# A hybrid token mixer on one core: TensorE's order in the recurrent scan phase written out by a merge of two instruction streams

## The chip, the cores and the metric

The kernel runs on one core of a Trainium2 chip. The metric is the device time of one execution in microseconds (us), as the median of several runs. The engines are TensorE (PE, with its weight loads as PEld), VectorE (DVE), ScalarE (ACT), GpSimd (POOL) and SyncE (SP), which issues the DMA transfers. Each engine takes its instructions strictly in the order in which they stand in the program; what a program fixes is that order and the semaphores that an instruction waits for.

## What is computed

Two layers of a diffusion backbone on 256 latent and 256 context tokens of width 1024, in float32. Each layer runs a half-step SwiGLU, three token mixers side by side (grouped attention, a bidirectional RWKV-7 recurrence, a 2-D neighbourhood attention) whose outputs are gated and merged, and another half-step SwiGLU. The change touches the recurrence:

```python
def rwkv_scan(state0, xs, emit):
    def step(state, inp):
        r_t, w_t, k_t, v_t, a_t, b_t = inp
        sa = jnp.einsum('zbhvk,zbhk->zbhv', state, a_t)
        state = state * w_t[..., None, :] + sa[..., :, None] * b_t[..., None, :] + v_t[..., :, None] * k_t[..., None, :]
        out = jnp.einsum('zbhvk,zbhk->zbhv', state, r_t) if emit else None
        return state, out
    return lax.scan(step, state0, xs)
```

z is the direction (forward, backward), h one of 8 heads of size 64. The context is scanned first, and its final state starts the scan of the latent tokens. In the last layer only the latent outputs are needed.

## The kernel before, in words

The large products (feed-forward, input projection, output projection) are "dense": a float32 product is made of three float32r matmuls of 128x128 weights on 512 or 256 columns (`gemm`, L272 to L274; the same in `quantum`, L773 to L775). These three are called a triple below. ACT and DVE split each loaded weight tile into a high and a low part first (L262, L263).

The mixer of a layer has a **scan phase** (`rwkv`) and an attention phase behind it. In the scan phase the 8 heads are taken as 4 columns of two heads (ct = 0 to 3). For each column there are four stages, each of which needs the one before:

- **prep** (`rwkv_prep`, `rwkv_dir`, `gram`): projections of k, v, r for the column (`proj`, tiles `ps_p`), then for each of the two directions a chain over ACT, POOL and DVE from two small products (`ps_w` L949, `ps_a` L953) to the gram products (`ps_g` L1041) and transposes (`ps_kb` L1011 to L1018).
- **inverse** (`inverse`): blocks of 16x16 are inverted on DVE after a transfer to DRAM and back, then five groups of small products for each direction widen that to 64x64 (`ps_x`, `ps_it`, `ps_iw` in `mm` L1127, and `ps_x`, `ps_w` at L1146, L1154).
- **chain** (`chain_steps`): 8 chunk steps, one after the other; in each, PE makes `ps_z` (L1182), ACT copies it, PE makes `ps_u` (L1203), ACT and DVE copy it, PE makes `ps_h` (L1210), DVE adds it into the next state. Products for the outputs (`ps_oo`, L1191 and L1224) stand beside that. Each of these groups is 4 matmuls of 64 columns; a float32 matmul shows as two records in the trace, so a group is x8.
- **out** (`rwkv_out`): normalisation of the column's output over POOL and DVE, and its gate (`ps_gg` L1241).

To fill PE beside this, `spare_quanta` makes a list of 336 **quanta** of the other input projections (tile `ps_gate`); one quantum is one triple, and 8 make a tile. `fill(n)` writes the next n into the program. 64 quanta in layer 0 and 16 in layer 1 (`LEFT`) are kept for the attention phase. The table `FILL` says after which column how many tiles are written. Within layer 0 all dense matmuls of the phase are on 512 columns; in layer 1, 720 of the 960 of `ps_gate` are on 256.

The order on each engine is set by a scheduler that simulates the program and takes, among what is ready in its simulation, what was written first; `prio` moves a block ahead or behind. The chain has `prio(-30)`, and the fill is written last, so it is ready all the time and goes wherever PE would wait, also into the middle of a group of four.

Of the kernel before, what the change touches and what calls it, by code (L numbers as in the profile page):

```python
# [43 lines left out]
FILL = [[5, 7, 3, 4, 24], [8, 5, 4, 4, 24]]  # L44
# [7 lines left out]
    0, 4, 5, 6, 10, 14, 18, 19, 20, 21, 25, 29, 33)  # L52


class Program:
# [261 lines left out]
    def rstd(self, sqs, n, cols, scale, eps, tag="aux"):  # L317
# [5 lines left out]
        for k, sq in enumerate(sqs):  # L323
            for b in range(n):
# [5 lines left out]
                                in1=self.mhalf[:, 0:n * w].rearrange("p (n w) -> p n w", n=n), op=ALU.pow)  # L330
        bc = self.bank(tag, [P, n * P], "ps_bc")
# [193 lines left out]
    def proj(self, tile_i, full):  # L525

        nc = self.nc
        pt = self.bank("mm", [P, NT], "ps_p")
        for h in range(2):
# [273 lines left out]
    def fill(self, n):  # L803

        for _ in range(min(n, len(self.fq))):
            self.fq.pop(0)()


    def shift(self, i, full, pt=None):

        nc, l = self.nc, self.l
        if pt is None:
            pt = self.proj(T_R + i, full)
# [16 lines left out]
    def rwkv(self):  # L830
# [25 lines left out]
        for h in HALVES:  # L856
            for w, pt in zip(ws, pts):
# [5 lines left out]
        self.gdt = self.shift(T_GD - T_R, tok)  # L863
        nc.scalar.activation(out=self.gdt[:, tok], in_=self.gdt[:, tok], func=AF.Tanh, scale=0.5)
        nc.vector.tensor_scalar(out=self.gdt[:, tok], in0=self.gdt[:, tok], scalar1=0.5, scalar2=0.5,
                                op0=ALU.mult, op1=ALU.add)
        self.fq = self.spare_quanta()
        self.fill_to = self.rp, "gm"
        st = {}
# [19 lines left out]
        self.fill(len(self.fq) - 8 * LEFT[l])  # L889
        return y  # L890

    def rwkv_prep(self, ct, st):
# [6 lines left out]
        pk, pv = self.kv0 if ct == 0 else (None, None)  # L899
        k = self.shift(T_RK - T_R + ct, FULL, pk)  # L900
        yield
        v = self.shift(T_RV - T_R + ct, FULL, pv)
        yield
        r = self.shift(ct, tok)
        yield
        sq = self.t()
        nc.scalar.activation(out=sq, in_=k, func=AF.Square, scale=pr[:, 4, ct:ct + 1])
        bc = self.rstd([sq], 4, self.hsel, 1.0, 1e-12)
# [3 lines left out]
        yield  # L912
# [9 lines left out]
        for p in range(2):  # L922
# [3 lines left out]
            nc.vector.tensor_copy(X[o, :, 1, p, :], pv[o, ::-1, :])  # L926
        st["X"] = X
# [6 lines left out]
        st["bonus"] = bonus  # L934
        st["z"] = []
        for z in range(2):
            yield
            st["z"].append((yield from self.rwkv_dir(ct, z, r, k, kk, lora)))

    def rwkv_dir(self, ct, z, r, k, kk, lora):  # L940
# [10 lines left out]
        nc.scalar.activation(out=sw, in_=pw, func=AF.Tanh, scale=0.5, bias=self.wah[:, l, z, ct:ct + 1])  # L951
        pa = self.bank("aux", [P, NT], "ps_a")
# [18 lines left out]
        yield  # L971
# [25 lines left out]
        yield  # L997
        G = self.gram(z, bk, ar)
        yield
# [6 lines left out]
        for p in range(2):  # L1006
# [15 lines left out]
            kb.append(t)  # L1022
        return dict(ar=ar, kb=kb, G=G, pc=pc)

    def gram(self, z, bk, ar):
# [6 lines left out]
        for jh in (1, 0):  # L1032
# [10 lines left out]
            for p in range(2):  # L1043
# [3 lines left out]
                G[p][jh] = g  # L1047
        return G

# [9 lines left out]
    def inverse(self, dirs):  # L1059
# [40 lines left out]
        for i, t in ((0, R), (1, N)):  # L1100
            nc.sync.dma_start(out=dr[i].rearrange("j z (g s) t -> (j z g) (s t)", s=16), in_=t)
        for z in range(2):
# [29 lines left out]
            nc.scalar.activation(out=X, in_=px, func=AF.Copy)  # L1132
            pt = mm("ps_it", W, X)
            nc.vector.tensor_tensor(out=T, in0=T, in1=pt, op=ALU.add)
            pw = mm("ps_iw", X, W)
            nc.vector.tensor_tensor(out=W, in0=W, in1=pw, op=ALU.add)

# [11 lines left out]
            for p, eng in ((0, nc.scalar), (1, nc.vector)):  # L1149
                self.copy(eng, X[rows(p, b)], px[rows(p, b)])  # L1150
            pw = self.bank("ia", [P, NCH, 32], "ps_w2")
# [12 lines left out]

    def rwkv_chain(self, ct, st):
        po = self.bank("po", [P, NCH, C], "ps_oo")
        return po, self.chain_steps(st, po)

    def chain_steps(self, st, po):
# [5 lines left out]
        for s in range(NCH):  # L1175
# [4 lines left out]
            for z, p in units:  # L1180
                rows = halves[1 - p] if first else slice(0, P)
                ins = nc.tensor.matmul(zp[halves[p], z, :], dirs[z]["G"][p][js[z] // 4][rows, js[z] % 4, 0:C],  # L1182
                                       X[rows, s, z, p, :], start=True, stop=True)
            yield ins
# [264 lines left out]
```

## Time and profile before

| | |
|---|---|
| median of 3 runs | 2931.0 us (2927.77 to 2934.51) |
| the profiled execution's own time | 2933.89 us, of which its span is 2932.1 us |
| mean granted TensorE clock | 0.971 |
| PE busy in the span | 2795.4 us (95%) |
| scan phase of layer 0 | about 463 to 995 us of the span |
| scan phase of layer 1 | about 2118 to 2541 us of the span |

The profile is of one execution. Times in its rows are microseconds from the start of the span; a row of the timeline merges equal instructions that follow each other. Matmuls are pipelined and their ends are modelled, so what one costs is read from start to start, not from its duration. "PEclk" is the granted share of TensorE's full clock: 1.0 is 2.4 GHz, 0.5 is 1.2 GHz.

### The profile page before, as it was taken

To read this page: it belongs to the slowest core of one execution; us is meant where nothing else is said; L and a number is where in the kernel's file an instruction comes from. 1 tells how busy PE (TensorE), PEld (TensorE's weight loads), DVE (VectorE), ACT (ScalarE), POOL (GpSimd) and SP (SyncE) were. 2 spreads that over 40 slices of the span, in tenths; PEclk is the share of its full clock that TensorE was granted. 3 is DMA by queue.
4 is the path that set the end of the run, shared out by engine and by line. 5 is a ranking of instruction groups with operands and counts; after the bars stand their busy time and mean duration, and the time that the engine had idled before them with its cause. 6 is when DMAs were issued, how large, how long until landed. Compare 5 with 4: busy or idle time off the path is not lost. (4 is left out here: it accounts for less than half of the span.)

```text
span 2932.1 us, 48565 instructions
## 1 busy us (share of the span) xinstructions
PE 2795.4 (95%) x19654; PEld 2229.4 (76%) x19654; DVE 1766.0 (60%) x3023; ACT 1068.6 (36%) x1928; POOL 277.6 (9%) x274
## 2 busy tenths in 40 slices
PE   7999999999999899999999999999899999898998
PEld 5788887656666666697888888888876678777998
DVE  4667346756674256757673477633578777485654
ACT  3223235323232246433222333222543433374543
POOL 0000011100000111230000110001210110022000
PEclk8999999999999999999999999999999999799998
DMA  7555343221112433336553365433432224344654
GB/s 277 201 187 170 107 134 105 76 69 44 41 58 73 133 108 110 105 119 215 171 181 106 119 201 183 147 102 107 141 114 69 70 60 119 104 130 138 218 177 144
DMA packets 205311, 376.59 MB, mean 128 GB/s; under 512 B 79776, under 2 KB 109088, under 8 KB 205088
## 3 DMA queue, kind: packets, MB, share of 16 engines
q1 hardware_dynamic: 205088, 373.51, 41.1%
q8 instruction: 154, 2.52, 0.4%
q14 instruction: 69, 0.57, 0.1%
HBM read 340.93 MB, written 31.46 MB: 127 GB/s over the span
## 5 line engine op out<-in xcount | busy, mean ns | idle before, releaser
L262 ACT ACTIVATE whi<-raw 128x1024 fp32r<-128x1024 f32 (+1 forms) x399 | 415.1, 1041 | 1102.5 <-PE ps_o L273 297.5
L263 DVE TENSOR_TENSOR wlo<-raw,whi 128x1024 fp32r<-128x1024 f32 (+1 forms) x399 | 500.4, 1255 | 425.1 <-ACT whi L262 415.8
L195 DVE SCALAR_TENSOR_TENSOR acc<-araw,cs,acc 128x1024 f32<-128x1024 f32 x210 | 260.6, 1279 | 14.3 <-DMA araw<-in_w_ada 14.0
L272 PE MATMUL ps_o<-hh,whi 128*128 128x512 f32 (+1 forms) x770 | 268.8, 349 | 0.0
L274 PE MATMUL ps_o<-hh,wlo 128*128 128x512 f32 (+1 forms) x770 | 268.0, 348 | 0.0
L273 PE MATMUL ps_o<-hl,whi 128*128 128x512 f32 (+1 forms) x770 | 266.6, 346 | 0.0
L272 PE MATMUL ps_fg<-uh,whi 128*128 128x512 f32 (+1 forms) x704 | 255.4, 363 | 7.3 <-ACT whi L262 3.7
L773 PE MATMUL ps_gate<-uh,whi 128*128 128x512 f32 (+1 forms) x672 | 255.6, 380 | 3.1 <-ACT whi L262 3.1
L274 PE MATMUL ps_fu<-uh,wlo 128*128 128x512 f32 (+1 forms) x704 | 251.9, 358 | 5.1 <-DVE wlo L263 5.1
L774 PE MATMUL ps_gate<-ul,whi 128*128 128x512 f32 (+1 forms) x672 | 256.0, 381 | 0.0
L274 PE MATMUL ps_fg<-uh,wlo 128*128 128x512 f32 (+1 forms) x704 | 253.4, 360 | 1.7 <-DVE wlo L263 1.7
L775 PE MATMUL ps_gate<-uh,wlo 128*128 128x512 f32 (+1 forms) x672 | 254.4, 379 | 0.7 <-DVE wlo L263 0.6
L273 PE MATMUL ps_fg<-ul,whi 128*128 128x512 f32 (+1 forms) x704 | 252.7, 359 | 0.1
L272 PE MATMUL ps_fu<-uh,whi 128*128 128x512 f32 (+1 forms) x704 | 251.2, 357 | 0.9 <-ACT whi L262 0.9
L273 PE MATMUL ps_fu<-ul,whi 128*128 128x512 f32 (+1 forms) x704 | 250.9, 356 | 0.0
L272 PEld LDWEIGHTS ps_fg<-uh,whi 128*128 128x128 f32 x704 | 134.8, 191 | 38.3 <-ACT whi L262 12.0
L272 PEld LDWEIGHTS ps_o<-hh,whi 128*128 128x128 f32 x770 | 144.7, 188 | 20.4 <-ACT whi L262 1.7
L273 PEld LDWEIGHTS ps_o<-hl,whi 128*128 128x128 f32 x770 | 144.5, 188 | 20.1
L274 PEld LDWEIGHTS ps_o<-hh,wlo 128*128 128x128 f32 x770 | 144.7, 188 | 18.2
L274 PEld LDWEIGHTS ps_fu<-uh,wlo 128*128 128x128 f32 x704 | 133.7, 190 | 26.6 <-DVE wlo L263 8.0
L773 PEld LDWEIGHTS ps_gate<-uh,whi 128*128 128x128 f32 x672 | 130.2, 194 | 28.3 <-issue 5.7
L274 PEld LDWEIGHTS ps_fg<-uh,wlo 128*128 128x128 f32 x704 | 134.7, 191 | 22.2 <-DVE wlo L263 3.0
(298 smaller groups left out, 5270.2 us busy)
## 6 DMA issues: line engine op xcount, KB each, us to landing
raw<-in_ffn_wi SPq DMA_DIRECT2D x176, 512.0 KB, 3.6
araw<-in_w_ada SPq DMA_DIRECT2D x144, 512.0 KB, 3.8
raw<-in_w_in SPq DMA_DIRECT2D x92, 512.0 KB, 3.7
raw<-in_ffn_wo SPq DMA_DIRECT2D x70, 448.0 KB, 3.3
raw<-in_ffn_wo SPq DMA_DIRECT2D x35, 512.0 KB, 3.5
pd<-fg SPq DMA_DIRECT2D x52, 256.0 KB, 2.0
raw<-in_w_branch SPq DMA_DIRECT2D x24, 512.0 KB, 3.8
praw<-in_w_in SPq DMA_DIRECT2D x44, 256.0 KB, 2.8
```

Source lines behind the costliest of these rows:

```text
L195: nc.vector.scalar_tensor_tensor(out=a, in0=raw, scalar=c, in1=a, op0=ALU.mult, op1=ALU.add)
L262: nc.scalar.activation(out=hi[:, :m], in_=r, func=AF.Copy)
L263: self.lo = nc.vector.tensor_tensor(out=lo[:, :m], in0=r, in1=hi[:, :m].bitcast(F32), op=ALU.subtract)
L272: nc.tensor.matmul(pt, wh, xh[k], start=first and k == 0, stop=False)
L273: nc.tensor.matmul(pt, wh, xl[k], start=False, stop=False)
L274: nc.tensor.matmul(pt, wl, xh[k], start=False, stop=last and k == n - 1)
L773: nc.tensor.matmul(pt, wh, xh, start=k == 0, stop=False)
L774: nc.tensor.matmul(pt, wh, xl, start=False, stop=False)
L775: nc.tensor.matmul(pt, wl, xh, start=False, stop=k == KD - 1)
```

## The change

`rwkv` no longer writes prep, chain and fill one after the other for a scheduler to mix. Two generators, `chains` (chain and out of the columns in turn) and `preps` (projections, prep and inverse of the columns in turn), stop (`yield`) after each whole group of matmuls and say two numbers: what the group costs PE, and how long after it the next group can start. `Streams.step` keeps a clock `t` of the program from these numbers. It takes the chain's next group if its time has come, else the preparation's, else one quantum of the fill; only if the fill has run out does it move the clock on. For the PE alone, a `manual_schedule` block makes the order in which the code writes the order on the engine; the other engines are ordered by the scheduler as before. `FILL` is gone; `LEFT` is as it was. A column's prep waits until the chain two columns back is done; the projections of the next column go beside the chain, a triple at a time. In `rwkv_out` the square goes to the buffer `fg` in place of `t`, and the chain's blocks have priority 200.

```diff
+class Streams:
+    NEAR = 0.3
+    def step(self, streams):
+        live = [g for g in streams if self.ready.get(g, 0.0) is not None]
+        if not live:
+            return False
+        g = next((g for g in live if self.ready.get(g, 0.0) <= self.t + self.NEAR), None)
+        if g is None and self.fill(1):
+            self.t += self.cost
+            return True
+        if g is None:
+            g = min(live, key=lambda g: self.ready[g])
+        self.t = max(self.t, self.ready.get(g, 0.0))
+        try:
+            cost, after = next(g)
+        except StopIteration:
+            self.ready[g] = None
+            return True
+        self.t += cost
+        self.ready[g] = self.t + after
+        return True
...
@@ proj
-            w = [[t[:, P * k:P * k + P] for k in range(4)] for t in (wh, wl)]
-            self.gemm(pt[:, full], w, [t[:, full] for t in self.uh[4 * h:4 * h + 4]],
-                      [t[:, full] for t in self.ul[4 * h:4 * h + 4]], h == 0, h == 1)
+            for k in range(4):
+                c, m = slice(P * k, P * k + P), 4 * h + k
+                self.gemm(pt[:, full], [[wh[:, c]], [wl[:, c]]], [self.uh[m][:, full]], [self.ul[m][:, full]],
+                          m == 0, m == KD - 1)
+                yield cost, 0.0
@@ rwkv
-        for _ in self.rwkv_prep(0, st):
-            pass
-        self.inverse(st["z"])
-        self.fill(8 * FILL[l][0])
-        for ct in range(4):
-            nxt = {}
-            po, chain = self.rwkv_chain(ct, st)
-
-            if ct < 3:
-                for _ in self.rwkv_prep(ct + 1, nxt):
-                    pass
-                self.inverse(nxt["z"])
-            with self.prio(-30):
-                for _ in chain:
-                    pass
-            self.rwkv_out(ct, st, po, y)
-            self.fill(min(8 * FILL[l][1 + ct], len(self.fq) - 8 * LEFT[l]))
-            st = nxt
+        left = 8 * LEFT[l]
+        mix = Streams(lambda n: len(self.fq) > left and self.fill(n), 0.69 if need else 0.45)
...
+            for ct in range(4):
+                yield from self.rwkv_proj(ct, sts[ct])
+
+                while done["chain"] < ct - 2:
+                    yield 0.0, 0.5
+                yield from self.rwkv_prep(ct, sts[ct])
+                yield from self.inverse(sts[ct]["z"])
+                done["prep"] = ct
...
+        streams = [chains(), preps()]
+        with self.tc.manual_schedule(engines={mybir.EngineType.PE}):
+            while mix.step(streams):
+                pass
@@ rwkv_dir (ahead of the gram products)
-        yield
-        G = self.gram(z, bk, ar)
-        yield
+        yield 1.1, 14.0
+        G = yield from self.gram(z, bk, ar)
@@ inverse (behind the transfers to DRAM)
+        yield 0.0, 20.0
@@ inverse (behind each of the first three groups; two more have 0.8, 1.0)
+            yield 1.15, 1.0
@@ chain_steps (behind ps_z, ps_u, and ps_h with ps_oo)
+            yield (0.45, 0.8) if first else (0.9, 0.4)
...
+            yield 0.45, 0.9
...
+            yield (0.9, 1.0) if out else (0.45, 1.4)
```

In the order below, a row is an instruction: its line, its tiles and the size of its output, with a count where equal ones follow each other. PE in layer 0, in the chain of the first column, before: a stretch of one chunk step.

```order
L1203 MATMUL ps_u<-zs,W 64x64
L773 MATMUL ps_gate<-uh,whi 128x512
L774 MATMUL ps_gate<-ul,whi 128x512
L1041 MATMUL ps_g_4748<-ar,bk 64x128 x8
L775 MATMUL ps_gate<-uh,wlo 128x512
L1210 MATMUL ps_h<-X,kb 64x64
L773 MATMUL ps_gate<-uh,whi 128x512
L1210 MATMUL ps_h<-X,kb 64x64
L774 MATMUL ps_gate<-ul,whi 128x512
L1210 MATMUL ps_h<-X,kb 64x64
L1041 MATMUL ps_g_4749<-ar,bk 64x128 x8
```

The last `ps_u` of a step, three of its `ps_h`, and gram products of the next column's prep alternate with single dense matmuls. The same column's chain in the changed kernel (its lines are other numbers):

```order
L1261 MATMUL ps_z<-X,G 64x64 x4
L1269 MATMUL ps_oo<-ar,X 64x64 x4
L305 MATMUL ps_p<-uh,phi 128x512
L306 MATMUL ps_p<-ul,phi 128x512
L307 MATMUL ps_p<-uh,plo 128x512
L1282 MATMUL ps_u<-zs,W 64x64 x4
L305 MATMUL ps_p<-uh,phi 128x512
L306 MATMUL ps_p<-ul,phi 128x512
L307 MATMUL ps_p<-uh,plo 128x512
L1289 MATMUL ps_h<-X,kb 64x64 x4
L1302 MATMUL ps_oo<-G,X 64x64 x4
```

Groups are whole, and dense matmuls come by threes. Counted over a scan phase (from its first `ps_first` to its last `ps_gg`), PE leaves the dense matmuls for small ones 305 times before and 114 times now in layer 0, 187 and 110 times in layer 1.

PE at the end of layer 0's scan phase, before: the last steps of the last column's chain.

```order
L1182 MATMUL ps_z<-X,G 64x64 x4
L1191 MATMUL ps_oo<-ar,X 64x64 x3
L773 MATMUL ps_gate<-uh,whi 128x512
L1203 MATMUL ps_u<-zs,W 64x64 x4
L774 MATMUL ps_gate<-ul,whi 128x512
L775 MATMUL ps_gate<-uh,wlo 128x512
L1224 MATMUL ps_oo<-G,X 64x64
L773 MATMUL ps_gate<-uh,whi 128x512
L1210 MATMUL ps_h<-X,kb 64x64 x4
```

Fill stands between all groups there, and 130 dense matmuls stand behind the last `ps_gg`. The same place in the changed kernel, from the inverse of the last column into its chain:

```order
L1205 MATMUL ps_x<-it 64x64 x16
L1205 MATMUL ps_it<-it,W 64x64 x16
L1205 MATMUL ps_iw<-W,it 64x64 x16
L1227 MATMUL ps_x_8188<-it,G 32x32 x16
L1236 MATMUL ps_w_8208<-W,it 32x32 x16
L1261 MATMUL ps_z<-X,G 64x64 x4
L1282 MATMUL ps_u<-zs,W 64x64 x4
L1289 MATMUL ps_h<-X,kb 64x64 x4
L1302 MATMUL ps_oo<-G,X 64x64 x4
L1261 MATMUL ps_z<-X,G 64x64 x4
```

No dense matmul stands in that row. The fill is used up 39 dense matmuls into the inverse of the third column in layer 0, and 27 dense matmuls into the second direction of the third column's prep in layer 1. From there only the projections beside the third column's chain are left: 160 small matmuls in a row ahead of that chain and 497 behind it in layer 0, 209 and 465 in layer 1.

## Rows read from the trace of the kernel before

**Rows 1.** Windows, both scan phases: start:end, us, PE, PEld, DVE, ACT, POOL busy, PEclk, DMA

```profile
463.00:995.00 532.00, 516.06 (x4637) 354.49 (x4635) 317.14 (x703) 171.46 (x332) 43.46 (x30) 0.99 0.23 67
2118.00:2541.00 423.00, 395.70 (x4463) 308.39 (x4462) 306.74 (x697) 168.58 (x338) 39.43 (x30) 0.95 0.30 85
```

**Rows 2.** Timeline, PE, layer 0: start us, us, engine, line, operation; one group broken up

```profile
637.28 0.39 PE L773 MATMUL ps_gate<-uh,whi 128*128 128x512 f32 x1
637.60 0.32 PE L1203 MATMUL ps_u<-zs,W 64*64 64x64 f32 x2
...
640.24 0.39 PE L775 MATMUL ps_gate<-uh,wlo 128*128 128x512 f32 x1
640.47 0.39 PE L773 MATMUL ps_gate<-uh,whi 128*128 128x512 f32 x1
```

**Rows 3.** Timeline, PE, layer 0: a whole group between dense matmuls

```profile
775.21 0.40 PE L274 MATMUL ps_p<-uh,plo 128*128 128x512 f32 x1
775.54 0.45 PE L1203 MATMUL ps_u<-zs,W 64*64 64x64 f32 x8
...
776.25 0.39 PE L774 MATMUL ps_gate<-ul,whi 128*128 128x512 f32 x1
```

**Rows 4.** Timeline, PE, layer 1: dense matmuls on 256 columns

```profile
2500.18 0.28 PE L775 MATMUL ps_gate<-uh,wlo 128*128 128x256 f32 x1
2500.39 0.33 PE L1203 MATMUL ps_u<-zs,W 64*64 64x64 f32 x2
...
2500.87 0.28 PE L774 MATMUL ps_gate<-ul,whi 128*128 128x256 f32 x1
2500.99 0.29 PE L775 MATMUL ps_gate<-uh,wlo 128*128 128x256 f32 x1
```

**Rows 5.** Timeline, PE: first column's prep, layer 0 (three rows) and layer 1

```profile
484.66 1.02 PE L953 MATMUL ps_a<-sh,lora 64*128 64x512 f32 x2
...
496.31 0.89 PE L1041 MATMUL ps_g<-ar,bk 64*64 64x128 f32 x24 [1.33 <-DVE bk L996]
...
527.58 0.22 PE L1018 MATMUL ps_kb<-c_ident,bk 64*64 64x64 f32 x1
...
2131.09 1.02 PE L953 MATMUL ps_a<-sh,lora 64*128 64x512 f32 x2
...
2172.28 0.22 PE L1018 MATMUL ps_kb<-c_ident,bk 64*64 64x64 f32 x1
```

**Rows 6.** Timeline, PE: an inverse's first product (layer 0; layer 1, first and third column)

```profile
555.92 0.32 PE L1127 MATMUL ps_x<-it 64*64 64x64 f32 x2
...
2202.04 0.33 PE L1127 MATMUL ps_x<-it 64*64 64x64 f32 x2
...
2367.45 0.22 PE L1018 MATMUL ps_kb<-c_ident,bk 64*64 64x64 f32 x1
...
2382.42 0.33 PE L1127 MATMUL ps_x<-it 64*64 64x64 f32 x2
```

**Rows 7.** Timeline, PE and DVE: products of the inverse in layer 0

```profile
562.22 1.15 PE L1127 MATMUL ps_iw<-W,it 64*64 64x64 f32 x32
...
563.41 0.69 DVE L1136 TENSOR_TENSOR W<-W,ps_iw 128x512 f32<-128x512 f32 x1 [1.45 <-PE ps_iw L1127]
...
564.35 0.69 PE L1146 MATMUL ps_x<-it,G 32*32 32x32 f32 x32
```

**Rows 8.** Window and timeline, layer 1: the end of the last chain, without fill

```profile
2520.00:2524.00 4.00, 3.64 (x46) 3.03 (x42) 1.87 (x7) 0.55 (x2) 0.00 (x0) 0.50 0.02 8
...
2518.43 0.70 PE L1182 MATMUL ps_z<-X,G 128*64 128x64 f32 x8
2522.44 0.70 PE L1182 MATMUL ps_z<-X,G 128*64 128x64 f32 x8
```

**Rows 9.** Timeline, layer 1: from the chain's end to the attention phase's first product

```profile
2533.71 0.39 ACT L1232 ACTIVATE yf<-ps_oo 128x256 f32<-128x256 f32 x1 [1.11 <-PE ps_oo L1224]
...
2540.66 0.58 PE L272 MATMUL ps_b<-yh,whi 128*128 128x256 f32 x1 [0.52 <-DVE yf L1242]
```

More of the change, by code (lines that the diff above doesn't have):

```diff
@@ L52, with __init__ @@
     0, 4, 5, 6, 10, 14, 18, 19, 20, 21, 25, 29, 33)
+class Streams:
+    NEAR = 0.3
+    def __init__(self, fill, cost):
+        self.t = 0.0
+        self.fill, self.cost = fill, cost
+        self.ready = {}
+    def step(self, streams):
[17 more added lines that the diff above has]
+        return True
 class Program:
@@ L315, in stats_add, with rstd, rstd_steps @@
             nc.gpsimd.tensor_tensor(out=self.zs[:, h], in0=self.zs[:, h], in1=self.z[m][:, h], op=ALU.add)
-    def rstd(self, sqs, n, cols, scale, eps, tag="aux"):
+    def rstd(self, *args, **kw):
+        steps = self.rstd_steps(*args, **kw)
+        while True:
+            try:
+                next(steps)
+            except StopIteration as e:
+                return e.value
+    def rstd_steps(self, sqs, n, cols, scale, eps, tag="aux", after=3.2):
         nc = self.nc
@@ L330, in rstd @@
                                 in1=self.mhalf[:, 0:n * w].rearrange("p (n w) -> p n w", n=n), op=ALU.pow)
+        yield 1.1, after
         bc = self.bank(tag, [P, n * P], "ps_bc")
@@ L528, in proj @@
         pt = self.bank("mm", [P, NT], "ps_p")
+        cost = 0.69 if full is FULL else 0.36
         for h in range(2):
@@ L803, in fill, with shift @@
     def fill(self, n):
-        for _ in range(min(n, len(self.fq))):
+        n = min(n, len(self.fq))
+        for _ in range(n):
             self.fq.pop(0)()
-    def shift(self, i, full, pt=None):
+        return n
+    def shift(self, i, full, pt):
         nc, l = self.nc, self.l
-        if pt is None:
-            pt = self.proj(T_R + i, full)
         ns = (full.stop - full.start) // SEQ
@@ L889, in rwkv, with preps @@
-        self.fill(len(self.fq) - 8 * LEFT[l])
-        return y
+        sts = [{} for _ in range(4)]
+        done = {"prep": -1, "chain": -1}
+        mix = Streams(lambda n: len(self.fq) > left and self.fill(n), 0.69 if need else 0.45)
+        def preps():
+            pg = yield from self.proj(T_GD, tok)
+            self.gdt = self.shift(T_GD - T_R, tok, pg)
+            nc.scalar.activation(out=self.gdt[:, tok], in_=self.gdt[:, tok], func=AF.Tanh, scale=0.5)
+            nc.vector.tensor_scalar(out=self.gdt[:, tok], in0=self.gdt[:, tok], scalar1=0.5, scalar2=0.5,
+                                    op0=ALU.mult, op1=ALU.add)
+            for ct in range(4):
[5 more added lines that the diff above has]
+                done["prep"] = ct
@@ new lines, in chains @@
+        def chains():
+            for ct in range(4):
+                while done["prep"] < ct:
+                    yield 0.0, 0.5
+                with self.prio(200):
+                    po = self.bank("po", [P, NCH, C], "ps_oo")
+                steps = self.chain_steps(sts[ct], po)
+                while True:
+                    with self.prio(200):
+                        try:
+                            said = next(steps)
+                        except StopIteration:
+                            break
+                    yield said
+                yield from self.rwkv_out(ct, sts[ct], po, y)
+                done["chain"] = ct
@@ new lines, in rwkv, with rwkv_proj @@
+        streams = [chains(), preps()]
+        with self.tc.manual_schedule(engines={mybir.EngineType.PE}):
+            while mix.step(streams):
+                pass
+        self.fill(len(self.fq) - left)
+        return y
+    def rwkv_proj(self, ct, st):
+        tok = self.tok
+        pk, pv = self.kv0 if ct == 0 else (None, None)
+        if pk is None:
+            pk = yield from self.proj(T_RK + ct, FULL)
+        st["k"] = self.shift(T_RK - T_R + ct, FULL, pk)
+        if pv is None:
+            yield 0.0, 1.5
+            pv = yield from self.proj(T_RV + ct, FULL)
+        st["v"] = self.shift(T_RV - T_R + ct, FULL, pv)
+        yield 0.0, 1.5
+        pt = yield from self.proj(T_R + ct, tok)
+        st["r"] = self.shift(ct, tok, pt)
+        yield 0.0, 1.5
@@ L970, in rwkv_dir @@
             last = 0
-        yield
         inv = self.t()
@@ L1047, in gram @@
                 G[p][jh] = g
+            yield 1.7, 1.6
         return G
@@ L1243, in rwkv_out @@
         y.append(os_)
+        yield 1.05 if self.need else 0.5, 0.0
     def mixer(self, l, need, nxt_fn, then):
```

49 lines of the change are left out of this document (20 added, 29 removed).

## The prediction, made before the changed kernel ran

> **What bounds the kernel now.** I read the windows of the two scan phases first, since the change orders nothing else. PE is busy for 516.1 of 532 us in layer 0 and 395.7 of 423 in layer 1 [rows 1]: it waits for 15.9 and 27.3 us, and DVE, next, is busy for 317 and 307. So in these phases PE's own instruction stream sets the end, and the time is the price of that stream plus what it waits. The reader is to see two things next. The timeline shows what it costs PE to go from dense matmuls to a small one and back [rows 2 to 4]. And the rows of single stages show how long a column takes from prep to out when PE is not the limit [rows 5 to 9]; before, that hardly matters, since fill stands in every gap, up to the last column's out and behind it in layer 0.
>
> **What the change gives back: crossings.** A broken group: from 637.28 to 640.47, 3.19 us, PE does six dense matmuls and four single `ps_u` (the rows left out alternate in the same way) [rows 2]. Six dense at 0.23 each, the distance of the last two rows, are 1.38, so the four cost 1.81. A whole group: from 775.21 to 776.25, 1.04 us, it does two dense (0.46) and the same four `ps_u`, which so cost 0.58 [rows 3]. Three crossings less are worth 1.23, or 0.41 each. In layer 1, beside 256 columns, two dense at 0.12 and one `ps_u` take 0.69 from 2500.18 to 2500.87, so one single is 0.45, against a quarter of 0.58: 0.31 each [rows 4]. The order has 191 crossings less in layer 0 and 77 less in layer 1: 191 x 0.41 + 77 x 0.31 = 78 + 24 = 102 us. Bounds: 0.31 for all is 83, 0.41 for all 110. PE's waits of 15.9 and 27.3 go into the new sum as well and are taken off here, and some 5 us of layer 1, where the end of the last chain ran at a clock of 0.50 [rows 8] and stays as slow: 48. Together 150 us to gain, if PE never waited.
>
> **What the change takes: cover.** The dense matmuls are as many as before; the clock of the program only deals them out. It deals 60 to 87 of them into each gap that the code says (14 and 20 us), and then has none left: the whole last column and a part of the third run bare. PE waits out there what a column takes, less its own small matmuls, which are paid before as well.
>
> The last column, stage by stage. Prep, from the end of the first `ps_a` to the last `ps_kb`: 485.68 to 527.80, 42.1 us, and 2132.11 to 2172.50, 40.4 [rows 5]. PE did fill beside it, but the chain of ACT, POOL and DVE set these times, so 41. The transfer stage of the inverse, from that `ps_kb` to the first product: 28.1 and 29.5 in the first columns, where projections' splits stood in the same queues, 15.0 at the least (2367.45 + 0.22 to 2382.42), where its masks had run ahead [rows 5, 6]. Bare it has neither; I take 22, the middle. The products: ten groups, three of 1.15 and two of 0.69 for each direction, and after each a copy of 0.69 or two of less on DVE and ACT, with some 0.1 on either side [rows 7]: 10 x 2 = 20 (16 to 24). The chain: 8 steps of 4.01, 2518.43 to 2522.44 at a clock of 0.50, which is what a bare chain was granted, 1.2 GHz [rows 8]: 32. If it kept 2.4 GHz, the three groups on the path at 0.45 in place of 0.70 [rows 3, 8] would make it 26. Out: 2533.71 to 2540.66, 7 us [rows 9]. Sum 122 (104 to 135). PE's own part: 497 and 465 small matmuls in a row, at 1.15 / 16 = 0.072 each [rows 7], 36 and 33. So a last column costs 86 and 89 us of waiting: 175 in both layers.
>
> The third column. Layer 0: 39 dense x 0.23 = 9 us lie in the transfer gap of 22, 13 bare, and the products' 20 less 160 x 0.072 = 12, 8 bare: 21. Layer 1: the gap from `ps_a` to `ps_g` is 10.6 us [rows 5] and 27 x 0.12 = 3 lie in it, 7.5 bare; gram and transposes with no cover some 3.5 (an estimate: half of the 7 us that is left of 41 in each direction after gap and next `ps_a`); then 22 and 8: 41. Together 62.
>
> The joins, where a chain has ended, no projection is left and out waits for POOL: one bare out of 7 us in each layer beyond the last: 14.
>
> Covers that are too short where fill is still there. Layer 1, second column: 117 dense x 0.12 = 14 for 22, and 51 x 0.12 = 6.1 for 10.6: 12.5. Layer 0: 87 x 0.23 = 20 for 22, twice: 4. Together 17 (0 to 35).
>
> The chain's groups in three covered columns of two layers, 144 of them, each have a triple (0.70) or two ahead, and their copies stand on ACT and DVE behind the splits of the dense weights; a late copy now stops PE and all that is queued behind that group, the next triples too. The trace shows no such place for a whole group. Nothing at best; 0.3, half of a DVE operation of 0.69 [rows 7], at worst, 43 us. I take 0.1, since the triple outlasts one copy: 14. The square's move to the buffer of the fill's store costs nothing while out waits for POOL anyway, and at most the waits already in the joins. The projections that are cut into triples are the same matmuls.
>
> Sum: 175 + 62 + 14 + 17 + 14 = 282 us of new waiting, less 150: +132. The profiled execution took 2934, 3 above the median, so 2934 + 132 - 3 = 3063 us.
>
> **The rivals.** *The crossing costs more than its row, and the phase gets faster.* PE's weight loads are busy for only 354.5 of 532 and 308.4 of 423 us [rows 1]. If whole groups let PE run packed until the weight loads fill the phase, 178 + 115 = 293 us come back and not 150, and the sum is 2931 + 282 - 293 = 2920. It decides in favour of the change from (282 - 48) / 268 = 0.87 us for each crossing, or, at my 0.41 and 0.31, from a last column of about 56 us where I have 122. Against it stands that the rows price both sides of a crossing and leave no room for 0.87. For it: bare stages may be quicker than covered ones; at all low ends (104 for a last column, no stalls) new waiting is some 185, and 185 - 158 with the dear crossings is still +27. The Trainium skill, in "Perfetto Trace Analysis", section "Identifying the Most-Contended Engine", calls matmul busy time a bad measure of how far TensorE is from its limit and takes the share of the weight loads; by that rule the phases stand at 67% and 73% and this rival is what a good order could reach. The trace agrees so far that crossings hide in a PE that shows 97% busy in layer 0; it does not show that all of the rest can be had. Chance 0.08.
>
> *Stalls of the rigid order.* ACT, DVE and the DMA queue are still ordered by the scheduler's simulation, PE now by another clock. If each of the 144 covered groups waits 0.4 us for its copy and the 40 covered gaps ahead of gram and products another 1 us, 44 + 40 more: 3063 + 84 = 3147. For it: DVE is busy 60 to 73% of the phase [rows 1]. Against it: the gaps of 14 us are longer than the 10.6 of the row. Chance 0.15.
>
> *Half of the crossings' price stays.* A group's own switches, between its shapes, remain: then 51 come back and not 102, 3114. Chance 0.12.
>
> *No change.* The bare column overlaps better than its stages in a row (transfers of one direction beside the other's chain): new waiting 150, 2931. Chance 0.04.
>
> **How the numbers follow.** My forecast has 0.61. The likeliest is 3063. The range reaches from 2980, the low ends of column and transfer with my crossings, to 3150, the stalls included; it leaves out the faster and the unchanged case and what lies above the stalls, less than 2 in 10. Faster by over 0.2% (about what a measurement of this kernel can tell from no change) has 0.08, within 0.2% 0.04, slower 0.88.
>
> **What would show it.** In the trace of the changed kernel: PE full with triples of about 0.70 us between whole groups in the first two columns, and a single `ps_u` group costing about 0.6; then, near the end of either phase, a stretch of 120 us or more with no dense matmul, PE busy for about a third to a half of it, and a granted clock of 0.5 there; waits of PE for `bk`, for the transfers' masks and for the copies of chain and products, some 280 us in both phases. Layer 0's phase should end some 30 us later and layer 1's some 100 later. It is wrong if the last column's bare stretch is under 60 us, if the first two columns show waits in each step, or if triples between groups take longer than 0.70.

## The result and the profile after

The changed kernel takes 3135.9 us (3133.5 to 3138.4), the kernel before 2932.8 beside it: a ratio of 1.069 (95% interval 1.067 to 1.072), 203 us slower. The forecast was slower with 0.88, 3063 us, and 2980 to 3150: side and range hold, the likeliest time is 73 us short.

Two lines of the page of the changed kernel, busy time of PE in the span (us, share, instructions) and its granted clock in 40 slices:

```profile
PE 2785.3 (89%) x19654; PEld 2261.3 (72%) x19654; DVE 1764.4 (56%) x3023; ACT 1070.9 (34%) x1928; POOL 277.7 (9%) x274
...
PEclk9999999999875699999999899999998967589999
```

PE was busy for 95% of the span before. The clock falls to 5 to 7 tenths in slices 12 to 14 and 33 to 35: the ends of the two scan phases.

The phases in windows, the answer to [rows 1] (start:end, us, then busy time of PE, PEld, DVE, ACT, POOL, PEclk, DMA):

```profile
471.00:1060.00 589.00, 480.96 (x4588) 356.28 (x4586) 314.64 (x698) 170.88 (x329) 41.77 (x30) 0.83 0.20 60
2191.00:2748.00 557.00, 408.05 (x4449) 326.60 (x4448) 305.68 (x696) 168.90 (x337) 39.53 (x30) 0.79 0.22 65
```

PE is not busy for 108 and 149 us, where it was 16 and 27 [rows 1]. Counted from the start of the last `ps_first` to that of the first `ps_b`, the phases took 526.7 and 421.1 us before and take 588.7 and 557.0 now: +62 and +136, and +5 us lie elsewhere. The forecast had +30 and +100.

The same phases by stretch (chain 1; prep and inverse of column 2; of column 3, and its chain; the last column to the end; then layer 1: prep and inverse of column 2, its chain, prep and inverse of column 3, last column):

```profile
589.28:643.00 53.72, 53.22 (x499) 35.99 (x498) 30.82 (x77) 19.09 (x42) 5.21 (x3) 0.97 0.19 60
643.00:736.45 93.45, 87.81 (x762) 66.47 (x760) 52.89 (x105) 29.51 (x48) 5.02 (x5) 0.95 0.36 104
...
789.00:881.82 92.82, 68.43 (x655) 52.72 (x653) 50.66 (x105) 24.05 (x40) 4.52 (x5) 0.78 0.26 77
881.82:935.00 53.18, 47.27 (x462) 32.54 (x461) 26.96 (x69) 16.36 (x38) 5.24 (x3) 0.89 0.03 11
935.00:1060.00 125.00, 62.14 (x822) 49.06 (x821) 57.92 (x149) 19.84 (x47) 7.06 (x4) 0.50 0.05 7
...
2357.00:2455.00 98.00, 74.92 (x843) 66.55 (x843) 55.84 (x109) 32.18 (x55) 5.79 (x5) 0.84 0.38 112
2455.00:2501.00 46.00, 42.16 (x440) 30.97 (x439) 28.52 (x70) 17.68 (x43) 4.15 (x3) 1.00 0.21 64
2501.00:2585.00 84.00, 44.56 (x594) 38.41 (x592) 45.65 (x103) 19.68 (x37) 5.75 (x5) 0.63 0.19 50
...
2630.00:2748.00 118.00, 55.47 (x755) 43.32 (x756) 55.53 (x151) 20.24 (x50) 6.16 (x4) 0.50 0.05 8
```

The reader is to see three things. Where a chain has projections beside it, PE is full: 53.2 of 53.7 us. The last columns run at a clock of 0.50, and PE is busy for half of them. And between them, in the second and third columns, cover is already missing: 5.6, 24.4 and 5.9 us in layer 0, 23.1, 3.8 and 39.4 in layer 1.

A covered chain step and a bare one, PE's timeline in layer 0, as answers to [rows 2, 3] and to [rows 8]:

```profile
594.41 0.45 PE L1269 MATMUL ps_oo<-ar,X 64*64 64x64 f32 x8
594.79 0.50 PE L305 MATMUL ps_p<-uh,phi 128*128 128x512 f32 x1
...
595.68 0.45 PE L1282 MATMUL ps_u<-zs,W 64*64 64x64 f32 x8
596.06 0.50 PE L305 MATMUL ps_p<-uh,phi 128*128 128x512 f32 x1
...
596.95 0.45 PE L1289 MATMUL ps_h<-X,kb 128*64 128x64 f32 x8
597.24 0.40 PE L1302 MATMUL ps_oo<-G,X 128*64 128x64 f32 x8
```

```profile
1020.89 0.70 PE L1261 MATMUL ps_z<-X,G 128*64 128x64 f32 x8 [0.38 <-DVE X L1294]
...
1022.01 0.69 PE L1282 MATMUL ps_u<-zs,W 64*64 64x64 f32 x8
1023.40 0.69 PE L1289 MATMUL ps_h<-X,kb 128*64 128x64 f32 x8 [0.70 <-DVE X L1284]
...
1024.88 0.70 PE L1261 MATMUL ps_z<-X,G 128*64 128x64 f32 x8 [0.36 <-DVE X L1296]
```

The covered groups wait for nothing. From start to start, a triple between two groups takes 0.89 us (594.79 to 595.68) where three dense matmuls in a row take 0.70, and a group ahead of dense ones 0.38 where `ps_h` ahead of `ps_oo` takes 0.29: a whole crossing is some 0.28. A bare step takes 3.99 (1020.89 to 1024.88), and PE waits in it for the copies ahead of `ps_z` and `ps_h`.

The last column's transfer gap, the answer to [rows 5, 6] (PE's timeline in layer 0; it ends where PE has waited 18.16 us for `it`):

```profile
972.32 1.46 PE L1086 MATMUL ps_kb<-c_ident,bk 64*128 64x64 f32 x15 [2.66 <-DVE bk L1078]
...
992.35 0.47 PE L1205 MATMUL ps_x<-it 64*64 64x64 f32 x2 [18.16 <-DVE it L1198]
```

And what PE waits for in the phases (line waited at, releaser: us, times, longest), layer 0, then layer 1:

```profile
PE ps_x L1205 <- DVE it L1198: 36.4, 8, 18.2
PE ps_g L1117 <- DVE bk L1072: 15.7, 2, 10.0
PE ps_kb L1086 <- DVE bk L1078: 13.1, 8, 2.7
```

```profile
PE ps_x L1205 <- DVE it L1198: 48.8, 8, 18.2
...
PE ps_kb L1086 <- DVE bk L1078: 16.4, 8, 2.7
PE ps_gate L822 <- DVE wlo L296: 10.1, 4, 3.4
```

### The profile page after: what moved, and what is told of

It is laid out like the page before. It is cut to its first block, busy times and chain, and to the rows that moved or that the text cites. A ratio compares the mean times of both kernels' runs of the same rounds, so it can differ in the third digit from the quotient of the medians.

```text
span 3133.4 us, 48609 instructions
## 1 busy us (share of the span) xinstructions
PE 2785.3 (89%) x19654; PEld 2261.3 (72%) x19654; DVE 1764.4 (56%) x3023; ACT 1070.9 (34%) x1928; POOL 277.7 (9%) x274
## 5 line engine op out<-in xcount | busy, mean ns | idle before, releaser
L822 PE MATMUL ps_gate<-uh,wlo 128*128 128x512 f32 (+1 forms) x672 | 246.8, 367 | 13.6 <-DVE wlo L296 13.6
L821 PE MATMUL ps_gate<-ul,whi 128*128 128x512 f32 (+1 forms) x672 | 246.9, 367 | 0.0
L822 PEld LDWEIGHTS ps_gate<-uh,wlo 128*128 128x128 f32 x672 | 136.4, 203 | 34.5 <-DVE wlo L296 15.5
L307 PEld LDWEIGHTS ps_o<-hh,wlo 128*128 128x128 f32 x770 | 145.4, 189 | 18.2
```

Of the source, the lines that this page charges most:

```text
L307: nc.tensor.matmul(pt, wl, xh[k], start=False, stop=last and k == n - 1)
L821: nc.tensor.matmul(pt, wh, xl, start=False, stop=False)
L822: nc.tensor.matmul(pt, wl, xh, start=False, stop=k == KD - 1)
```

## The experiments

A table of the phases first, as defined above, from each kernel's profiled execution; ratios are to the kernel before, run beside it.

| kernel | layer 0, us | layer 1, us | median, us | ratio (95%) |
|---|---|---|---|---|
| before | 526.7 | 421.1 | 2933 to 2941 | 1 |
| changed | 588.7 | 557.0 | 3135.9 | 1.069 (1.067 to 1.072) |
| e1_broken | 618.3 | 580.7 | 3186.8 | 1.083 (1.079 to 1.088) |
| e2_spread | 594.2 | 577.1 | 3159.0 | 1.075 (1.070 to 1.080) |
| e3_ahead | 543.9 | 518.9 | 3050.7 | 1.038 (1.033 to 1.042) |
| e4_warm | 596.6 | 573.2 | 3153.7 | 1.073 (1.068 to 1.077) |
| e5_free | 556.3 | 496.0 | 3038.8 | 1.033 (1.031 to 1.035) |
| e8_pipe | 516.9 | 476.1 | 2981.0 | 1.014 (1.012 to 1.016) |
| e9_gap | 481.7 | 439.8 | 2903.1 | 0.990 (0.986 to 0.994) |
| e10_prio | 503.0 | 450.7 | 2937.2 | 1.000 (0.998 to 1.002) |
| e11_layer0 | 484.1 | 417.0 | 2889.1 | 0.983 (0.980 to 0.986) |
| e12_free | 476.6 | 412.8 | 2883.2 | 0.981 (0.979 to 0.983) |

**What a crossing costs (e1).** `self.three` holds the dense matmuls of the next triple; the loops over `ps_oo` in `chain_steps` take one after each of the first three:

```diff
+    def nick(self, n):
+        if self.three and (n or len(self.three) == 3):
+            self.three.pop(0)()
+            return n + 1
+        return n
@@ chain_steps, behind each ps_oo matmul
+                    broken = self.nick(broken)
```

> Groups broken up on purpose. In the covered chains of the changed kernel the four ps_oo of a group are taken apart by the dense matmuls of the next triple (o D o D o D o in place of o o o o D D D). Same matmuls, same place of every group that the chain waits for; only TensorE's switches between dense and small grow, by 70 in layer 0 and 30 in layer 1. Theory (the median start-to-start distances of all switches: 0.326 + 0.149 + 0.337 us, less two dense at 0.235 and one small at 0.07): a crossing costs 0.27 us, so +27 us, 3163. Rival (the price of the prediction, 0.41 and 0.31): +38 us, 3174. If a crossing cost 0.87, as the fast rival of the prediction needed: +87, 3223. If it cost nothing where the planner sets the order: 3136.

Layer 0's phase grew by 29.6 us for 70 crossings: 0.42 each, the price of the prediction; my lower one fell. The whole kernel got 51 us slower by the medians (41 by the ratios), for the 38 of that price; what is over lies in layer 1. PE's timeline of one broken group in layer 0:

```profile
595.03 0.28 PE L1312 MATMUL ps_oo<-G,X 128*64 128x64 f32 x2
595.24 0.49 PE L583 MATMUL ps_p<-uh,phi 128*128 128x512 f32 x1
595.67 0.33 PE L1312 MATMUL ps_oo<-G,X 128*64 128x64 f32 x2
...
597.04 0.33 PE L1312 MATMUL ps_oo<-G,X 128*64 128x64 f32 x2
597.30 0.50 PE L583 MATMUL ps_p<-uh,phi 128*128 128x512 f32 x1
```

From the first `ps_oo` to the dense matmul behind the last, 2.27 us. As a whole group and a whole triple, the same seven take 1.13 in the changed kernel (the step before the covered one above, 592.11 to 593.24), so it is 1.14 more for three crossings. A dense matmul that stands alone costs more than 0.28: its switch to the small ones took 0.43 (595.24 to 595.67), behind a run 0.32. Layer 1 grew by 23.7 for 30, which no such price explains (0.31 each would be 9). Two windows of covered chains of this kernel, layer 1 and layer 0:

```profile
2500.00:2525.50 25.50, 24.74 (x172) 18.76 (x168) 9.66 (x27) 4.92 (x13) 0.25 (x1) 0.60 0.11 32
...
749.00:796.00 47.00, 46.03 (x359) 28.36 (x357) 20.70 (x57) 12.85 (x29) 0.00 (x0) 1.00 0.14 46
```

PE is busy throughout, and yet in layer 1 the clock stood at 0.60 beside 256 columns, where the same chain with whole groups had 1.00 (2455 to 2501 above).

**Dealing the fill out (e2).**

```diff
+        share = (len(self.fq) - left) // 4
-        mix = Streams(lambda n: len(self.fq) > left and self.fill(n), ...)
+        mix = Streams(lambda n: len(self.fq) > left + share * max(0, 2 - done["prep"]) and self.fill(n), ...)
```

> The fill is dealt out by column: until the inverse of column n is done, no more than (n + 1) quarters of it may be used. Nothing else changes. Theory (demand: the columns stand one behind the other and need more cover than there is, so that cover given to the last column is missing in the others): the waits only move, the gain is what the first columns had too much, some 4 us in each covered gap, 0 to 40 us in all, 3096 to 3136. Rival (bad dealing: the loss is the bare last column, 87 us in each layer): at least 100 us come back, under 3036.

No gain: 1.075 against the 1.069 of the changed kernel, with intervals that meet, and both phases longer in the profile. The last columns, in windows:

```profile
931.00:1065.00 134.00, 97.96 (x992) 76.52 (x990) 68.02 (x160) 32.05 (x63) 6.61 (x4) 0.69 0.19 54
...
2640.00:2770.00 130.00, 79.39 (x949) 68.05 (x947) 65.58 (x160) 31.37 (x66) 6.47 (x4) 0.65 0.18 52
```

The clock is up from 0.50, but the last columns are longer (134 and 130 us for 125 and 118), with 168 and 192 dense matmuls in each. And the first column of layer 0, which gave away 114 of the 344 dense matmuls ahead of its chain, got no longer: that chain starts 115.0 us behind the last `ps_first`, 118.2 in the changed kernel. So dealing was not the fault. As far as this run shows, a column's time is its stages in a row, with cover or without, and cover only decides whether PE does other work meanwhile. The theory's side held, its small gain did not come.

**Projections a column ahead (e3).** Projections of the next column become a third stream that starts when the previous column's k, v, r are read; the second half of the keys waits for the running chain, whose buffers it needs:

```diff
-                yield from self.rwkv_proj(ct, sts[ct])
+        def projs():
+            for ct in range(1, 4):
+                while done["dirs"] < ct - 1:
+                    yield 0.0, 0.5
+                yield from self.rwkv_proj(ct, sts[ct])
+                done["proj"] = ct
@@ in front of the second ps_kb
+            while p == 1 and self.wait():
+                yield 0.0, 0.5
```

> The projections of the next column are a stream of their own that begins as soon as the previous column's k, v and r have been read, so they stand in the transfer gap of the inverse, and the next column's prep (its first direction, up to where the buffers of the running chain end it) goes beside the chain. Order on TensorE still whole groups, same planner, same fill. Theory (serial columns: the loss comes from a prep that starts only when the chain is over): some 20 us of each of three columns in both layers move under a chain, the fill lasts into the last column, and layer 0 comes near TensorE's own work of some 460 us, layer 1 near 440: 3136 - 97 - 112 = about 2927 (2890 to 2990). Rival (the rigid order itself stalls TensorE, another engine being late by its own order): more groups beside the chain, more stalls, 3060 or above.

3051: 45 and 38 us came back in the phases, less than half of what the theory wanted, and more than the rival allowed. The stretch without a dense matmul at a phase's end has shrunk, to 79 and 98 us from 144 and 132, and is not gone (last columns; layer 0: end of prep with inverse, then chain and out; layer 1: end of prep with inverse):

```profile
906.00:970.00 64.00, 43.19 (x502) 35.38 (x500) 32.94 (x75) 14.85 (x26) 1.30 (x1) 0.75 0.27 74
970.00:1013.00 43.00, 28.96 (x337) 22.98 (x333) 17.07 (x54) 7.56 (x23) 2.02 (x1) 0.50 0.01 1
2555.00:2613.00 58.00, 22.73 (x409) 19.36 (x409) 28.38 (x74) 8.02 (x19) 1.26 (x1) 0.50 0.13 25
```

**The clock (e4).** Junk triples, whose result nobody reads, where the fill is out and all projections are done:

```diff
+        if g is None and self.junk and self.junk():
+            self.t += 0.9
+            return True
```

> Junk triples: where the planner's fill has run out and all projections are done, a dense triple whose result nobody reads is put in its place, one for each 0.9 us that the planner would have moved its clock; all of the kernel's own work stays. It keeps the granted clock of TensorE up in the bare last column. Theory (a third of the last column's cost is the clock): products of the inverse 24.6 to 20 us, chain 31 to 28 (groups at 0.45 in place of 0.70, less what a triple delays them), some 10 us in each layer, 3110 to 3120. Rival (it is all waiting for other engines, the clock costs nothing or the triples cost as much as they give): 3130 to 3150.

No gain: 1.073 against 1.069; 3154 lies just above the rival's range. In the products of the last column's inverse the clock stood at 1.00 (first row, a window of layer 0), and they took 9.7 us from one direction's `ps_iw` to the next one's, where the bare ones took 12.2. But the chain, on its timeline (the other rows),

```profile
1003.30:1014.70 11.40, 10.75 (x211) 8.08 (x210) 4.85 (x10) 2.90 (x7) 0.00 (x0) 1.00 0.01 4
...
1023.80 0.45 PE L1274 MATMUL ps_z<-X,G 128*64 128x64 f32 x8
...
1024.56 0.96 PE L960 MATMUL ps_p<-uh 128*128 128x512 f32 x3
1025.45 0.45 PE L1295 MATMUL ps_u<-zs,W 64*64 64x64 f32 x8
...
1028.25 0.45 PE L1274 MATMUL ps_z<-X,G 128*64 128x64 f32 x8
```

takes 4.45 a step (1023.80 to 1028.25) with triples that stand in its way, 3.99 bare at half the clock. In the products the clock is worth some 5 us a layer (twice the 2.5); what the bare chain would take at 2.4 GHz, no run shows.

**The order on TensorE left to the scheduler (e5).**

```diff
-        with self.tc.manual_schedule(engines={mybir.EngineType.PE}):
-            while mix.step(streams):
+        while mix.step(streams):
```

> The changed kernel with its one block taken away that makes the written order TensorE's order; code, merge, planner, buffers and fill as in the changed kernel, but TensorE is ordered by the scheduler's simulation again. Crossings 144 and 114 in place of 114 and 110. Theory (the loss is in the merge: a column's prep is written behind the chain, and the fill is dealt out early; a scheduler that takes what was written first can't get it back): about as slow as the changed kernel, 3115 to 3165. Rival (the rigid order stalls TensorE, since the other engines are late against the program's clock): the scheduler takes what is ready in its place, some 84 us come back, 3050 or less.

97 us came back, as the rival said. But not as it said. The first two columns take what they took (layer 0: 116 and 53 us to the end of the first chain's stage against 118 and 54; then 92 against 93). Most of the gain is at the end: prep and inverse of the last column, behind the third chain, take 63 us in place of 82 in layer 0 and 43 in place of 80 in layer 1, 19 of the 32 us and 37 of the 61 that the phases gained, because much of them ran before. The rest is spread, some 15 us of it over the windows of layer 1's first three chains. The two windows, then PE's timeline in the third column's chain, layer 0:

```profile
924.00:987.00 63.00, 27.54 (x437) 23.10 (x435) 29.17 (x77) 8.17 (x19) 1.77 (x1) 0.50 0.08 13
2574.00:2617.00 43.00, 19.89 (x344) 16.60 (x345) 18.13 (x57) 6.17 (x15) 0.00 (x0) 0.50 0.09 13
...
871.43 1.12 PE L1025 MATMUL ps_w<-sh,lora 64*128 64x512 f32 x2
872.48 0.32 PE L1282 MATMUL ps_u<-zs,W 64*64 64x64 f32 x2
...
873.88 2.07 PE L1030 MATMUL ps_a<-sh,lora 64*128 64x512 f32 x2 [0.24 <-ACT t L1027]
875.88 0.69 PE L1289 MATMUL ps_h<-X,kb 128*64 128x64 f32 x8
```

`ps_w` and `ps_a` of the last column stand between a `ps_u` and a `ps_h` of the third chain. In the written order nothing of the last column's prep could pass the chain ahead of it. The dense matmuls last no longer here (163 and 172 us at the ends have none, for 144 and 132), so it is not more cover that won the time. So the rigid order costs mainly by whole columns, not by late copies: e3 and e5 win much the same time, one by writing the overlap, the other by not forbidding it.

**Three columns at once (e8, e9, e10).** Inverse and prep become streams of their own (the core of it; a stream that waits hands over its condition and no longer moves the clock):

```diff
+        def inverses():
+            for ct in range(4):
+                yield lambda: done["dirs"] < ct
+                yield from self.inverse(sts[ct]["z"], lambda: done["steps"] < ct - 1)
+                yield lambda: done["steps"] < ct - 1 or done["v"] < ct or done["keys"] < ct
+                yield from self.rwkv_late(ct, sts[ct])
+                done["prep"] = ct
...
-        streams = [chains(), preps()]
+        streams = [chains(), inverses(), preps(), projs()]
...
-tag="G", name="G", bufs=12
+tag="G", name="G", bufs=16
```

> The whole order written out so that columns overlap: four streams in place of two (chain of column c, inverse of column c + 1, prep of column c + 2, projections behind them), each still in whole groups and merged by the same clock on TensorE alone. For it the buffers of a second column are made (G 16, ar 8, kb 6) and paid by one X, three W and by projections that load into the fill's raw tiles; the second direction's keys, X and the bonus are made when the chain ahead is done. A waiting stream no longer moves the clock, a fill triple counts 0.69 or 0.36 by its columns, and three gaps follow the trace (11.5, 25 from the last gram products, 2.6). Crossings 130 and 135. Theory (serial columns, crossing 0.4 as in the runs with broken groups): no dense-free stretch of over 60 us is left, layer 0's scan phase takes 455 to 490 us (527 before, 589 in the changed kernel), layer 1's 400 to 430 (421, 557), so 2870 (2830 to 2920), faster than the kernel before. Rival (the rigid order is what costs): more groups beside each other make more stalls; over 2960.

2981: better than the changed kernel by 155, and short of the theory by 111, the larger part in layer 1 (476 for at most 430). The time is in the rival's range (over 2960), though the longest stretch without a dense matmul is 50 us, under 60 as the theory said. Buffers, loads and three gaps changed along with the overlap, and no run takes these apart. Its largest wait in layers 0 and 1:

```profile
PE ps_x L1238 <- DVE it L1231: 30.1, 10, 7.5
```

```profile
PE ps_x L1238 <- DVE it L1231: 33.6, 8, 10.2
```

The inverse's first products were written 25 us behind the last gram products; that stage took 32 to 37 (23 in the changed kernel's bare last column, 25 to 31 in nearly all of its others). That two columns now share DVE would explain it, but is not shown. e9 changes two numbers:

```diff
-        yield 0.0, 25.0
+        yield 0.0, 36.0
@@ rwkv_late, ahead of the chain
-        yield 1.1, 0.2
+        yield 1.1, 2.0
```

> The kernel with four streams, and two numbers of its planner changed after its trace: the gap from the last gram products to the inverse's first product 36 in place of 25 us (it measured 32 to 37 there, since the next column's prep now shares DVE with the inverse, and TensorE stood 30 and 34 us ahead of these products), and 2.0 in place of 0.2 us ahead of a chain, for X. Nothing else changes. Theory (with columns overlapped, what is left of the rigid order's cost are groups written too early, on which everything behind them waits): most of the 64 us at ps_x goes, some 20 come back as waits elsewhere: layer 0 about 490, layer 1 about 455, 2935 (2915 to 2960). Rival (the products set the chain's start, so a later place only moves the wait to another engine's chain): 2965 to 3000.

2903, better than expected: 78 us for two numbers, and for the first time faster than the kernel before. The phases in windows:

```profile
468.00:950.00 482.00, 453.06 (x4589) 331.47 (x4587) 312.30 (x699) 170.88 (x329) 42.29 (x30) 0.95 0.25 72
2068.00:2508.00 440.00, 392.92 (x4455) 309.08 (x4454) 301.79 (x696) 168.39 (x337) 40.58 (x30) 0.91 0.29 82
```

Layer 0 gains 45 us on the kernel before, layer 1 loses 19. The first products came later still, 37 to 42 us behind the gram products, and yet the phases got shorter: that fits an early place which costs PE's wait and not the column's time. e10 takes a gap of 30, the 2.0 of e9, and sets the inverse ahead of the prep on the other engines:

```diff
-        yield 0.0, 25.0
+        yield 0.0, 30.0
+                    with self.prio(100):
+                        said = next(steps)
```

> The kernel with four streams; the inverse's work on ACT, POOL and DVE is put ahead of the next column's prep (a priority of 100 in the scheduler's simulation), the gap to its first product is 30, and 2.0 us stand ahead of a chain. Theory (DVE is shared: two columns' work makes the transfer stage 32 to 37 us long, 23 bare and 27 under dense weights only): the stage falls to 27 to 30 and the waits at ps_x go without pushing the products back, so somewhat better than the later gap, 2915 to 2945. Rival (the stage is long because of the DMA round trip, which a priority can't shorten): the stage stays at 32 or more, waits of 15 to 30 us stay, 2950 to 2980.

2937, inside the theory's times, but its mechanism fell: the stage still took 35 to 37 us in layer 0 and 32 to 40 in layer 1. So setting the inverse ahead did not shorten it. A time between those of e8 and e9 fits the gap alone.

**Which layer, and is it the written order? (e11, e12).** e11 runs layer 0's phase as in e9 and layer 1's as before:

```diff
+                if need:
+                    self.__class__ = Planned
                 yf = self.rwkv()
+                self.__class__ = Program
```

> Layer 0's scan phase in the order with four streams and the gap of 36, layer 1's as in the kernel before (scheduler's order, its code and its FILL). Theory (the gain is crossings and hangs on how full of dense work a phase is: layer 0's phase took 482 us in the last order against 527 before, layer 1's 440 against 421): the better of the two in each layer, 2937 - 45 = about 2890, ratio 0.984 (0.980 to 0.988). Rival (layer 1's 19 us more came from what layer 0's new phase leaves behind, a lower clock or later loads, and not from layer 1's order): no better than the last kernel, ratio 0.990 or above.

2889, ratio 0.983 as expected; layer 1's phase took 417 us, so the 19 us that it lost in e9 came from its own order and not from what layer 0 left behind. e12 is e9 with the block of e5 taken away, 187 and 163 crossings in place of 132 and 138:

> The kernel with four streams and the gap of 36, with the one block taken away that makes the written order TensorE's order: streams, buffers, dealing of the fill and priorities stay, TensorE is ordered by the scheduler's simulation. Crossings 187 and 163 in place of 132 and 138. Theory (the gain over the kernel before is the fewer crossings; an order on TensorE that the planner sets keeps them few): 55 + 25 crossings more at 0.4 and 0.3 us are some 30 us, less up to 15 us of waits that a scheduler avoids by taking what is ready: 2915 to 2935, ratio about 0.998, slower than with the written order (0.990). Rival (the gain is the overlap and the second column's buffers; the written order is a cost, as in the changed kernel): faster than with the written order, ratio 0.985 or less.

My theory fell a second time in the same place: 0.981 against 0.990, with more crossings 26 us faster by the ratios and 20 by the medians. Against e11's 0.983 it is no clear difference. Its phases:

```profile
467.00:944.00 477.00, 466.15 (x4590) 331.64 (x4588) 312.52 (x699) 171.69 (x329) 43.36 (x30) 0.99 0.26 73
2068.00:2481.00 413.00, 387.14 (x4448) 302.78 (x4446) 305.04 (x696) 167.93 (x337) 37.78 (x30) 0.95 0.31 88
```

PE waits for 11 and 26 us, in e9 for 29 and 47; it is busy 13 us longer in layer 0, 6 less in layer 1, at a clock of 0.99 and 0.95 for 0.95 and 0.91. Both phases are shorter than before (477 for 527, 413 for 421), with 187 and 163 crossings for 305 and 187. Weight loads are busy for 332 of 477 and 303 of 413 us there, 70 and 73%. By the rule of the Trainium skill that the prediction named ("Perfetto Trace Analysis", section "Identifying the Most-Contended Engine") PE would still have room; no run here used more of it.

## Why the prediction was right, and where it fell short

- **Crossings, 102 us back: right as far as measured.** e1, which puts crossings in, measured 0.42 in layer 0 for the 0.41 of [rows 2, 3]; for layer 1's 0.31, 24 of the 102 us, no run gives a clean price, since the clock fell there. The rivals that rested on a dearer or a cheaper crossing (0.87, or half of the price staying) don't fit 0.42. That triples would take 0.70 between groups was wrong, one of the signs by which the prediction called itself wrong: 0.89, with a run's own crossing in it.
- **Last column, 175: right.** Layer 0, from the end of the first `ps_a` to that of `ps_gg`, 929.6 to 1059.1, is 129.5 us for the 122 of the sum; layer 1 took 120. Less PE's own 36 and 33, 94 and 87: 180. Stage by stage in layer 0: prep 45 for 41, transfer gap 18.2 for 22, products 24.6 for 20, chain 31 for 32, out 11 for 7. The clock was 0.50, as said. (The prediction's 15.0 for the shortest transfer stage is 14.75 by its own rows; nothing hangs on it.)
- **Chain groups, 14: less.** Ahead of the groups of layer 0's first chain PE idles 0.06 us and 6.3 us ahead of those of all six covered chains together.
- **The first three columns: the step that was too small.** The sum gave them 62 + 14 + 17 + 14 = 107. With crossings at their price, 203 + 150 = 353 us are new, less 180 for the last columns 173. Of these, PE's idle time in the windows is 45 in layer 0 and 86 in layer 1; the rest, some 40, is mostly PE's own work at a lower granted clock (0.78 and 0.63 in the prep and inverse of the third columns), which the sum counted at full clock, with the 5 us outside. In these columns PE was busy for some 133 us at a clock of 0.50, in both whole phases of the kernel before for 49; if all of the 84 more took twice their time, 42 us are lost by it (an estimate, no run isolates it). Two waits were not in the sum for covered columns: at `ps_kb`, where the second scaling of `bk` is done on DVE 2.5 us or more behind the gram products and the code allows 1.6 (13.1 and 16.4 us over eight places in a layer, 5.3 of each in the last column), and in the fill itself, whose split came late in layer 1 (10.1). And the covers were too short from layer 1's first column on (PE idle for 10.3 of 119 us up to its chain and 3.0 in it), where I had none.
- **The rivals.** "Stalls of the rigid order" gave 3147, nearly the time. Half of its mechanism is there, a wait at many gaps; the other half, a late copy in each chain group, is not. e5 and e12 show what it missed: a written order costs 97 and 20 to 26 us here. In e5 the timeline shows why, a later column's ready work that could not pass; for e12 the mechanism is not shown. The range had its upper end from these stalls, and what filled it was covers too short and a low clock: that 3136 still lies inside is in part luck.
- **Where and when.** Layer 1 lost twice what layer 0 did, as said (+136 and +62 for +100 and +30). The bare stretches of 125 and 118 us at the phases' ends are there, and PE waits for 257 us in both phases where the text looked for some 280. That PE would be full in the first two columns held in layer 0's two chains (0.5 and 1.5 us idle) and not in the stretches between the chains.
- **Not taken apart.** The chain's priority of 200 and the square's buffer were taken back in no run. e12 has both and beats the kernel before, so they don't carry the loss alone.

## What to carry to other kernels

Price an order by the cover that it deals out, column by column, and not by the switches it saves: here some 100 us of saved switches came back, and some 300 us of waiting and of work at a low clock came with them (the 203 lost and those 100). If a latency chain repeats, write the next round's start beside this round's end before you fix anything; then let the scheduler place single instructions, or give each gap at least its measured length, since one gap that was some 10 us too short, and a small one beside it, cost 78 us. Fill that ends early was a sign of serial stages here, and spreading it only moved the waits.

## What the hardware showed beyond that

The granted clock fell with PE hardly waiting. In e1's layer 1 PE was busy for 24.7 of 25.5 us with single 256-column matmuls between single small ones and some whole triples, at a clock of 0.60; in the changed kernel, with the same matmuls in triples between whole groups, it was 1.00 (2455 to 2501), and in e1 beside 512 columns, broken as well, 1.00 (749 to 796). What decides between them was not tried.
